# Two passes for a head's output, four softmax scalings on ScalarE, low parts in the taps' queue, late loads and a tail by halves

## The chip, the core and the metric

The kernel runs on one core of a Trainium2 chip: TensorE for matmuls, VectorE, ScalarE, GpSimd and SyncE, with 16 DMA engines between HBM and the core's SBUF. The metric is the device time of one execution in microseconds; less is better.

## The reference

A decoder layer for 512 tokens of width 1024, all in fp32: a gated causal convolution of width 31 and a forgetting attention of 16 heads of 64 side by side, mixed by two gates, then a PEER layer that picks 16 of 16384 experts for each of 8 heads, then a final RMSNorm.

```python
h  = rmsnorm(x, norm1_g)
z  = h @ w_in            # a_val, a_gate, q, k, v, f_logit, g_a, g_b
ya = conformer_conv(a_val, a_gate, conv_w, conv_b, conv_ln_g, conv_ln_b, w_conv_out)
c  = cumsum(log_sigmoid(f_logit + fox_bf))
p  = softmax(where(mask, q @ k.T / 8 + c_q - c_k, NEG));  ob = p @ v      # 16 heads, causal
x  = x + (sigmoid(g_a) * ya + sigmoid(g_b) * (ob @ w_fox_out)) @ w_out
x  = x + peer_ffn(rmsnorm(x, norm2_g), peer_wq, peer_k1, peer_k2, peer_u, peer_v)
return rmsnorm(x, normf_g)
# peer_ffn: u = peer_u[e];  a = gelu(u . h) * gate;  out = sum_k a_k * peer_v[e_k]
```

## The kernel before

An fp32 operand is split into a high and a low part (`hi`, rounded to the matmul's fp32r type, and `lo`, the rest), and `mm3` (L170 to L172) does a product as three matmuls: high by low, low by high, high by high. Weights stream from HBM through SyncE's queue as `wraw`; ScalarE writes `whi` (L125), VectorE subtracts to `wlo` (L129). Every engine works through its instructions in the order in which the program issues them.

The stages, in the time of the profile: v and the first norm (0 to 66 us); the first GLU, q and k (66 to 92); attention (92 to 340); gates and the rest of the convolution (340 to 429); layer norm, output projections and queries (429 to 675); the u stage, 128 blocks of experts, each 24 matmuls of 384 columns (675 to 1269); the v stage, 128 blocks of 18 matmuls of 512 columns (1269 to 1801); and the tail.

Attention goes by pairs of heads, j = 0 to 7, with a ninth round for what is left. In round j the scores of pair j (L594 to L596), the row maxima `mx` (L600, VectorE), the exponentials (L602, ScalarE) and the scaling of the probabilities `Pt` by `rl` (`norm`, L606 to L612: the blocks listed in `NACT` on ScalarE, the others on VectorE) alternate with the transposes of pair j-1 (`tp` L623, split into `pth` on ScalarE and `ptl` on VectorE, L628 and L629) and its outputs (`pvmm`). In between `fill` puts projection steps of round j+1 (q and k in `qk_steps`, the GLU in `glu_steps`). What follows a matmul on other engines is put off by one step through the list `posts`. The convolution's 240 multiply-adds `y` (L493, the taps) are VectorE's background work: `tick` adds a rate per step (`ATT_R`, `ATT_R0`, `GB_R`) and `bg` issues a tap for each whole unit. Behind attention the taps left over run beside the gates (`GB0` steps), up to the sum of `y` that L756 takes.

In the u stage, `bgrun` hands out VectorE time to two generators after each block: routing with its scatter (one-hot tiles `ohs`, 16 small matmuls for each tile at L1066, copied to `gst` by ScalarE at L1069 and written to `Gd` in HBM), and the gathers of single expert rows (`grow`, first 128 products at L1100, then 128 sums at L1106, `U_BG` us a block). `open_second` drains the scatter, frees its memory and issues the first two loads of G, `load_g` (L1161), on ScalarE's queue. In the v stage the gathers left are spread over the blocks; a pair of blocks takes a product and a split of the coefficients (`a_pair`: L1182, `ah` L204, `al` L206).

Of the kernel before, what the change touches and what calls it, by code (L numbers as in the profile page):

```python
# [16 lines left out]
ALU = mybir.AluOpType  # L17
# [44 lines left out]
U_BG = 1.25  # L62
# [7 lines left out]
NACT = (2, 3)  # L70
# [4 lines left out]
VAHEAD = 9  # L75
GB8 = 8
# [9 lines left out]
def body(ctx, tc, x, xT, w_ct, w_v, w_f, w_co, w_fo, w_o, w_q, keys, pu, pv, pur, vecs, conv_w,  # L86
# [315 lines left out]
    def first(*fs):  # L402
        def fn():
            for f in fs:
# [6 lines left out]
                   first(norm1_row, lambda: next(n1)), first(lambda: next(n1))]  # L411
# [139 lines left out]
    def qk_steps(j):  # L551
# [3 lines left out]
        def qsink(p):  # L555
# [3 lines left out]
            def low():  # L559
                for r, u, f in zip(half, half[::-1], range(2)):  # L560
                    dve.scalar_tensor_tensor(qa[u, f, :], p[r, :], 1.0 / math.sqrt(HD), qa[r, f, :].bitcast(F32),
                                             op0=ALU.mult, op1=ALU.subtract)
                    pool.dma_start(qb[r, f, :], qa[r, f, :])
            posts.append(low)

        def ksink(p):
# [3 lines left out]
            def low():  # L570
                for r, u, f in zip(half, half[::-1], range(2)):
                    dve.tensor_tensor(kb[j % 2][r, f, :], p[r, :], ka[r, f, :].bitcast(F32), op=ALU.subtract)
                    pool.dma_start(ka[u, f, :], ka[r, f, :])
            posts.append(low)
# [763 lines left out]
```

## Time and profile before

| | before |
|---|---|
| median of 3 runs | 1814.32 us (1809.08 to 1818.4) |
| profiled execution | 1813.74 us, its span 1811.5 us |
| TensorE busy | 1759.0 us, 97% |
| VectorE busy | 1507.1 us, 83% |
| ScalarE busy | 876.6 us, 48% |
| GpSimd busy | 395.4 us, 22% |
| bytes moved by DMA | 432.92 MB, mean 239 GB/s |

The span is what the profiler saw from the first instruction to the last; the execution's time has some 2 us around it. Busy shares are means over stages with different limits. A row of a timeline gives the start, the duration, the engine, the line of the code, what is written from what, and in brackets how long the engine stood idle before it and which instruction released it. PE is TensorE, DVE VectorE, ACT ScalarE, POOL GpSimd, SP SyncE. The ends of matmuls are modelled and overlap the next one's start, so the distance between starts is what a matmul costs.

### The profile page before, as it was taken

The page shows a single profiled execution, that of the slowest core. Times are in us where ns is not written, and L with a number is a line of the kernel's source. Part 1 is how long each engine was busy: PE and PEld are TensorE (multiplying, and loading weights), DVE is VectorE, ACT ScalarE, POOL GpSimd, SP SyncE. Part 2 cuts the span into 40 slices and gives each one's busy share as a digit, 9 for nine tenths or more (in the row PEclk, how much of TensorE's full clock was granted, in tenths as well). Part 3 has the DMA queues.
Part 4 walks back from the last instruction along what each step waited for, and adds up shares of the span by engine and source line. Part 5 has one row for each costly group of instructions (what it writes and reads, how often), then busy time and mean ns, then how long its engine had stood idle before and what let it go on. Part 6 is the DMA issues. An engine that isn't in the chain of part 4 may idle for free.

```text
span 1811.5 us, 25347 instructions
## 1 busy us (share of the span) xinstructions
PE 1759.0 (97%) x9261; PEld 1537.6 (85%) x9261; DVE 1507.1 (83%) x2649; ACT 876.6 (48%) x1621; POOL 395.4 (22%) x303
## 2 busy tenths in 40 slices
PE   7999999999999999999999999998999999999997
PEld 6887777787888889999999999998888888788886
DVE  5789999999756599989987987865888888888887
ACT  5665655534624233344379489973333333333333
POOL 0000000000000000013422331224444444344441
PEclk9999999999999999999999999999999999999999
DMA  6332222222344225568889989999999999999994
GB/s 210 110 94 76 82 76 72 69 81 94 105 139 136 72 71 159 173 234 305 301 297 332 327 306 334 325 341 375 377 377 378 388 373 389 362 360 391 373 336 159
DMA packets 164477, 432.92 MB, mean 239 GB/s; under 512 B 13696, under 2 KB 63488, under 8 KB 162304
## 3 DMA queue, kind: packets, MB, share of 16 engines
q1 hardware_dynamic: 111408, 238.58, 38.2%
q0 software_dynamic: 39424, 138.43, 21.3%
q10 hardware_dynamic: 13520, 54.29, 7.9%
q8 instruction: 73, 1.20, 0.3%
q14 instruction: 52, 0.43, 0.1%
HBM read 376.20 MB, written 50.86 MB: 236 GB/s over the span
## 4 chain that ended last, share of the span: by engine, by line
PE 68%; DVE 16%; ACT 8%; DMA 6%; issue 3%; ACTq 0%; SPq 0%; POOL 0%; DVEq 0%
PE mm L170 19%; PE mm L171 19%; PE mm L172 19%; DVE y L493 4%; DVE wlo L129 3%; DMA wraw<-in_pv 2%; ACT whi L125 2%; PE tp L171 2%; PE tp L172 2%; PE tp L170 2%; PE pvp L1066 2%; DVE x L1106 2%; ACT ohs L1057 1%; DMA wraw<-in_pu 1%; DVE ptl L629 1%
## 5 line engine op out<-in xcount | busy, mean ns | idle before, releaser
L129 DVE TENSOR_TENSOR wlo<-wraw,whi 128x1024 fp32r<-128x1024 f32 (+1 forms) x434 | 432.5, 1004 | 98.1 <-ACT whi L125 94.4
L125 ACT ACTIVATE whi<-wraw 128x1024 fp32r<-128x1024 f32 (+1 forms) x429 | 373.9, 892 | 100.4 <-DMA wraw<-in_pv 38.9
L170 PE MATMUL mm<-h2h,wlo 128*128 128x384 f32 (+1 forms) x1152 | 398.1, 346 | 8.3 <-DVE wlo L129 7.7
L171 PE MATMUL mm<-h2l,whi 128*128 128x384 f32 (+1 forms) x1152 | 392.8, 341 | 0.5 <-DVE h2l L206 0.5
L172 PE MATMUL mm<-h2h,whi 128*128 128x384 f32 (+1 forms) x1152 | 393.0, 341 | 0.0
L1087 POOL DMA_INDIRECT grow<-in_pur,sx x128 | 181.8, 1421 | 602.5 <-DVE grow L1100 351.8
L1087 POOL DMA_INDIRECT grow<-in_pv,sx x128 | 190.0, 1484 | 236.7 <-DVE x L1106 219.6
L170 PEld LDWEIGHTS mm<-h2h,wlo 128*128 128x128 f32 x1152 | 216.9, 188 | 13.8 <-DVE wlo L129 8.4
L171 PEld LDWEIGHTS mm<-h2l,whi 128*128 128x128 f32 x1152 | 217.0, 188 | 5.7 <-DVE h2l L206 1.1
L172 PEld LDWEIGHTS mm<-h2h,whi 128*128 128x128 f32 x1152 | 216.7, 188 | 5.4
L171 PE MATMUL mm<-wlo,ah 128*128 128x512 f32 x512 | 202.1, 395 | 1.8 <-DVE wlo L129 1.7
L170 PE MATMUL mm<-whi,al 128*128 128x512 f32 x512 | 200.0, 391 | 1.1 <-DVE al L206 1.1
L172 PE MATMUL mm<-whi,ah 128*128 128x512 f32 x512 | 200.1, 391 | 0.0
L204 ACT ACTIVATE ah<-Sb 128x768 fp32r<-128x768 f32 x60 | 50.8, 846 | 292.8 <-DVE Sb L1182 264.6
L493 DVE SCALAR_TENSOR_TENSOR y<-z,cw,y 128x512 f32<-128x512 f32 x240 | 174.6, 746 | 1.0 <-ACT y L490 0.2
L1106 DVE SCALAR_TENSOR_TENSOR x<-grow,dots,x 128x1024 f32<-128x1024 f32 x128 | 164.2, 1283 | 0.9
L170 PE MATMUL mm<-hTh,wlo 128*128 128x512 f32 x384 | 161.7, 421 | 2.2 <-ACT Pt L602 1.6
L1100 DVE SCALAR_TENSOR_TENSOR grow<-grow,hd 128x1024 f32<-128x1024 f32 x128 | 155.2, 1217 | 0.8 <-DMA grow<-in_pur,sx 0.8
L172 PE MATMUL mm<-hTh,whi 128*128 128x512 f32 x384 | 151.1, 393 | 0.0
L171 PE MATMUL mm<-hTl,whi 128*128 128x512 f32 x384 | 150.5, 392 | 0.0
L1141 ACT ACTIVATE gel<-mm 128x384 f32<-128x384 f32 x118 | 57.4, 487 | 172.9 <-PE mm L172 108.2
L1057 ACT ACTIVATE ohs<-ohs,gl 128x128 f16<-128x128 f16 x384 | 118.8, 438 | 11.4 <-DVE ohs L1052 11.3
(280 smaller groups left out, 2914.5 us busy)
## 6 DMA issues: line engine op xcount, KB each, us to landing
wraw<-in_pu SPq DMA_DIRECT2D x128, 512.0 KB
wraw<-in_pv SPq DMA_DIRECT2D x128, 512.0 KB
wraw<-in_w_ct SPq DMA_DIRECT2D x48, 512.0 KB
Gd<-gst SPq DMA_DIRECT2D x24, 1024.0 KB
G<-Gd ACTq DMA_DIRECT2D x16, 1536.0 KB
Sb<-Sd ACTq DMA_DIRECT2D x60, 384.0 KB
Sd<-gel SPq DMA_DIRECT2D x59, 384.0 KB
wraw<-in_w_q SPq DMA_DIRECT2D x16, 512.0 KB
```

Source lines behind the costliest of these rows:

```text
L125: nc.scalar.activation(hi[:, nh * q:hi_to * q], raw[:, nh * q:hi_to * q], AF.Copy)
L129: eng.tensor_tensor(lo[:, c], raw[:, c], hi[:, c].bitcast(F32), op=ALU.subtract)
L170: nc.tensor.matmul(o, ll, rh, start=first, stop=False)
L171: nc.tensor.matmul(o, lh, rl, start=False, stop=False)
L172: nc.tensor.matmul(o, lh, rh, start=False, stop=last)
L204: nc.scalar.activation(hi, src, AF.Copy, scale=1.0 if scale is None else scale)
L493: dve.scalar_tensor_tensor(acc, z[:, w:w + S], cw[:, j, w:w + 1], acc, op0=ALU.mult, op1=ALU.add)
L1057: nc.scalar.activation(o[:, 3, g, :, t], o[:, 1, g, :, t], AF.Copy, scale=gl32[:, t0 + u:t0 + u + 1])
L1087: pool.indirect_dma_start(out=t, out_offset=None, in_=src, in_offset=bass.IndirectOffsetOnAxis(ap=sx[:, n % NG:n % NG + 1], axis=0))
L1100: yield 1.25, dve.scalar_tensor_tensor(t, t, 1.0, hd, op0=ALU.mult, op1=ALU.mult, accum_out=dots[:, k:k + 1])
L1106: yield 1.28, dve.scalar_tensor_tensor(o, t, dots[:, k:k + 1], o, op0=ALU.mult, op1=ALU.add)
L1141: nc.scalar.activation(gel[c][:, n, :], p[:, :TD], AF.Gelu_apprx_tanh)
```

## The change

Six edits, all in one program.

1. v is stored as one tensor `vv` in which a head's 64 high and 64 low columns stand side by side. `pvmm` multiplies each block of it by `ptl` and by `pth`: two matmuls for each of four key blocks instead of three. The output's upper and lower 64 rows have to be added: ScalarE copies one half (`other`), VectorE adds the other (`add`), and the pair's output is then split in one piece of 128 rows (`high` and a low part).
2. `NACT` lists all four blocks, so ScalarE does all scalings of `Pt`.
3. The low parts of q, k and of the output go into a list `lows` which `bg` empties ahead of the taps; `fill` runs the posts before the tick. Rates go from 1.06, 0.7 and 1.3 to 1.32, 0.95 and 1.4.
4. 14 matmuls of a constant stand at the program's start, and the first norm's row is moved one step later.
5. In the u stage `U_BG` goes from 1.25 to 1.15, one scatter tile is kept back while routing runs, and the loads of G and the extra gather buffers come four blocks after `open_second` (`VWAIT`).
6. The last two v blocks run merged by halves of a tile, with sums, scalings and stores by halves, and one half of the last tile is scaled on ScalarE.

```diff
-ATT_R = 1.06
-ATT_R0 = 0.7
+ATT_R = 1.32
+ATT_R0 = 0.95
-GB_R = 1.3
+GB_R = 1.4
-U_BG = 1.25
+U_BG = 1.15
-NACT = (2, 3)
+NACT = (0, 1, 2, 3)
+VWAIT = 4
...
+    wp = pv_ps()
+    for _ in range(NWARM):
+        nc.tensor.matmul(wp[:, :P], onesm, onesm, start=True, stop=True)
...
-                   first(norm1_row, lambda: next(n1)), first(lambda: next(n1))]
+                   first(), first(norm1_row, lambda: next(n1))]
...
+    lows = []
     def bg(n):
         for _ in range(n):
-            if not next(cg, False):
+            if lows:
+                lows.pop(0)()
+            elif not next(cg, False):
                 return
...
-    def pvmm(o, j, pth):
+    def pvmm(o, j, f, pth):
         for kb in range(NT):
             c = slice(OFFK[kb], OFFK[kb] + (NT - kb) * P)
-            mm3(o[:, kb * P:], (v_hi[:, j, kb, :], v_lo[:, j, kb, :]), (pth[0][:, c], pth[1][:, c]),
-                kb == 0, kb == NT - 1)
+            w = vv[:, j, kb, f].rearrange("p a c -> p (a c)")
+            for a in (1, 0):
+                nc.tensor.matmul(o[:, kb * P:], w, pth[a][:, c], start=kb == 0 and a == 1, stop=kb == NT - 1 and a == 0)
...
+        def high():
+            nc.scalar.activation(obT[0][:, j, :], t, AF.Copy)
+            lows.append(lambda: dve.tensor_tensor(obT[1][:, j, :], t, obT[0][:, j, :].bitcast(F32), op=ALU.subtract))
+        def add():
+            dve.tensor_tensor(t[r, :], o[half[0], :], t[r, :], op=ALU.add)
+            if f:
+                posts.append(high)
+        def other():
+            nc.scalar.activation(t[r, :], o[half[1], :], AF.Copy)
+            posts.append(add)
+        posts.append(other)
...
-                if next(gen, 1) is None:
-                    tick(0.65, rate)
+                more = next(gen, 1) is None
                 for fn in todo:
                     fn()
+                if more:
+                    tick(0.65, rate)
...
-        for g in range(GLD - 1):
-            load_g(g)
...
-        if later:
+        if len(later) > busy:
...
+        if vp and b == min(opened + VWAIT, NK - KEEP * SB2 + 1):
+            vready.append(1)
+            for g in range(GLD - 1):
+                load_g(g)
...
+    for i in range(1, NT):
+        k = slice((i - 1) * P, i * P)
+        for f, d in enumerate(halves):
+            for n, (hi, lo) in enumerate(wl):
+                mm3(oacc[i - 1][f], (ah[:, n, k], al[:, n, k]), (hi[:, d], lo[:, d]), False, n == SB2 - 1)
+            if f == 0:
+                scale(i - 1)
+            residual(i, f)
+            if i < NT - 1 and f:
+                for g in range(2):
+                    store(i - 1, g)
```

VectorE in the middle of an attention pair, from the reciprocal `rl` of a pair's first head on; before:

```order
L606 RECIPROCAL rl<-lsum 128x4
L612 TENSOR_SCALAR Pt<-Pt,rl 128x128
L612 TENSOR_SCALAR Pt<-Pt,rl 128x256
L493 SCALAR_TENSOR_TENSOR y<-z,cw,y 128x512
L600 TENSOR_REDUCE mx<-mm 128x1
L493 SCALAR_TENSOR_TENSOR y<-z,cw,y 128x512
L129 TENSOR_TENSOR wlo<-wraw,whi 128x512
```

and after, at the same place:

```order
L617 RECIPROCAL rl<-lsum 128x4
L611 TENSOR_REDUCE mx<-mm 128x1
L583 TENSOR_TENSOR kb<-mm,ka 64x512 x2
L131 TENSOR_TENSOR wlo<-wraw,whi 128x512
L501 SCALAR_TENSOR_TENSOR y<-z,cw,y 128x512
```

The two scalings are gone, the two low parts of k (`kb`), which stood ahead of `rl`, now stand behind it, and the taps have moved behind `wlo`.

ScalarE at the same place, from the high parts of k (`ka`) to the `whi` that `wlo` waits for; before:

```order
L568 ACTIVATE ka<-mm 64x512 x2
L610 ACTIVATE Pt<-Pt,rl 128x384
L610 ACTIVATE Pt<-Pt,rl 128x512
L580 ACTIVATE qb<-y,seld 64x512 x2
L125 ACTIVATE whi<-wraw 128x512
```

and after:

```order
L580 ACTIVATE ka<-mm 64x512 x2
L621 ACTIVATE Pt<-Pt,rl 128x128
L621 ACTIVATE Pt<-Pt,rl 128x256
L621 ACTIVATE Pt<-Pt,rl 128x384
L621 ACTIVATE Pt<-Pt,rl 128x512
L591 ACTIVATE qb<-y,seld 64x512 x2
L127 ACTIVATE whi<-wraw 128x512
```

Two more scalings stand ahead of `qb` and `whi`.

ScalarE around the first loads of G in the u stage, before:

```order
L1141 ACTIVATE gel<-mm 128x384
L1069 ACTIVATE gst<-pvp 128x128x4 x2
L1161 DMA G<-Gd 128x3072 x2
L125 ACTIVATE whi<-wraw 128x1024
L1141 ACTIVATE gel<-mm 128x384
```

and after:

```order
L1094 ACTIVATE gst<-pvp 128x128x4 x2
L127 ACTIVATE whi<-wraw 128x1024
L1166 ACTIVATE gel<-mm 128x384
L127 ACTIVATE whi<-wraw 128x1024
L1166 ACTIVATE gel<-mm 128x384
L127 ACTIVATE whi<-wraw 128x1024
L1166 ACTIVATE gel<-mm 128x384
L127 ACTIVATE whi<-wraw 128x1024
L1166 ACTIVATE gel<-mm 128x384
L1186 DMA G<-Gd 128x3072 x2
```

The two loads have moved behind four more blocks' `whi` and `gel`.

## Rows read from the trace of the kernel before

**Rows 1.** Busy time of each engine by stretch: the stretch in us, its length, then busy us (and instructions) of PE, PEld, DVE, ACT and POOL, the granted clock of TensorE as a share, DMA share and GB/s. An attention pair, the stretch behind attention, two stretches at the opening of the second stage, and the v stage.

```profile
199.19:233.13 33.94, 32.15 (x166) 25.80 (x165) 31.64 (x60) 20.13 (x46) 2.05 (x4) 1.00 0.27 77
340.30:428.90 88.60, 86.66 (x403) 71.80 (x401) 85.28 (x136) 32.61 (x59) 0.00 (x0) 1.00 0.23 78
...
1228.00:1238.00 10.00, 8.47 (x40) 8.47 (x41) 6.93 (x9) 3.36 (x6) 7.81 (x6) 0.76 0.98 385
1238.00:1269.00 31.00, 30.95 (x179) 30.63 (x178) 18.94 (x24) 10.80 (x15) 9.82 (x7) 1.00 1.02 409
1268.90:1800.60 531.70, 528.79 (x2305) 431.51 (x2304) 459.03 (x450) 180.24 (x200) 226.09 (x153) 1.00 0.95 359
```

**Rows 2.** The chain of waits over two attention pairs, 199 to 268 us: the shares by engine and line, then pieces as start, us, and what.

```profile
by line: DVE y L493 31.2%; DVE wlo L129 10.6%; DVE ptl L629 8.3%; DVE mx L600 7.4%; ACT Pt L610 5.4%; issue 4.3%; ACT qb L580 4.2%; DVE qa L561 4.0%; DVE v_lo L673 4.0%; DVE kb L572 3.8%; ACT qa L557 3.5%; ACT whi L125 3.4%; ACT v_hi L668 3
...
203.14 0.66 DVE y L493
...
233.13 1.23 ACT Pt L610 x2
```

**Rows 3.** VectorE's timeline at the two ends of a head's softmax, in mid-pair (198.92 to 202.45) and at a pair's end (214.31 to 216.50).

```profile
198.92 0.18 DVE L606 RECIPROCAL rl<-lsum 128x4 f32<-128x4 f32 x1
199.13 0.55 DVE L612 TENSOR_SCALAR Pt<-Pt,rl 128x128 f32<-128x128 f32 x2
...
202.45 0.69 DVE L129 TENSOR_TENSOR wlo<-wraw,whi 128x512 fp32r<-128x512 f32 x1 [1.12 <-ACT whi L125]
...
214.31 0.17 DVE L606 RECIPROCAL rl<-lsum 128x4 f32<-128x4 f32 x1
...
216.50 0.69 DVE L129 TENSOR_TENSOR wlo<-wraw,whi 128x512 fp32r<-128x512 f32 x1
```

**Rows 4.** ScalarE's timeline, the `whi` at the pair's end.

```profile
215.71 0.61 ACT L125 ACTIVATE whi<-wraw 128x512 fp32r<-128x512 f32 x1
```

**Rows 5.** ScalarE's groups in attention, 92 to 340.3 us, by shape: busy us, mean ns of one, and the idle time before them.

```profile
L610 ACT ACTIVATE Pt<-Pt,rl 128x512 f32<-128x512 f32 x15 | 10.6, 709 | 0.0
...
L610 ACT ACTIVATE Pt<-Pt,rl 128x384 f32<-128x384 f32 x15 | 9.3, 617 | 25.3 <-DVE rl L606 25.3
```

**Rows 6.** VectorE's groups of the same stretch.

```profile
L129 DVE TENSOR_TENSOR wlo<-wraw,whi 128x512 fp32r<-128x512 f32 x58 | 39.8, 687 | 10.5 <-ACT whi L125 10.3
...
L561 DVE SCALAR_TENSOR_TENSOR qa<-mm,qa 64x512 fp32r<-64x512 f32 x14 | 9.6, 689 | 2.7 <-ACT qa L557 2.6
...
L612 DVE TENSOR_SCALAR Pt<-Pt,rl 128x256 f32<-128x256 f32 x15 | 5.2, 348 | 0.0
...
L612 DVE TENSOR_SCALAR Pt<-Pt,rl 128x128 f32<-128x128 f32 x15 | 4.3, 287 | 0.5
```

**Rows 7.** TensorE's timeline: the first matmul of a head's output and the first matmul behind its twelve.

```profile
234.15 0.39 PE L170 MATMUL pvp<-pth,v_lo 128*128 128x512 f32 x1
...
236.00 0.39 PE L594 MATMUL mm<-ka,qa 128*128 128x384 f32 x1
```

**Rows 8.** TensorE's waits from 88 to 440 us: what waits, for what, us in total, times, longest.

```profile
PE tp L623 <- DVE ptl L629: 10.2, 7, 2.2
PE pvp L756 <- issue: 1.9, 1, 1.9
```

**Rows 9.** TensorE's timeline at the program's start.

```profile
7.13 0.77 PE L170 MATMUL mm<-whi,xgl 128*128 128x512 f32 x1 [7.13 <-DVE xgl L208]
...
10.78 0.40 PE L172 MATMUL mm<-whi,xgh 128*128 128x512 f32 x1
11.02 0.39 PE L170 MATMUL mm<-whi,xgl 128*128 128x512 f32 x1
...
31.62 2.08 PE L329 MATMUL tp<-ident,rsc 128*128 128x128 f32 x8 [3.12 <-POOL rsc L324]
```

**Rows 10.** TensorE's timeline in the u stage: the two sets of 16 one-hot matmuls of one block.

```profile
978.33 1.10 PE L1066 MATMUL pvp<-ohs 128*128 128x128 f16 x16 [0.86 <-ACT gst L1069]
...
983.98 1.10 PE L1066 MATMUL pvp<-ohs 128*128 128x128 f16 x16 [0.33 <-ACT gst L1069]
```

**Rows 11.** ScalarE's timeline at the opening of the second stage.

```profile
1226.29 0.83 ACTq L1161 DMA_DIRECT2D G<-Gd  x2
1227.16 1.06 ACT L125 ACTIVATE whi<-wraw 128x1024 fp32r<-128x1024 f32 x1 [13.04 <-issue]
```

**Rows 12.** TensorE's timeline there.

```profile
1229.53 0.69 PE L170 MATMUL mm<-h2h,wlo 128*128 128x384 f32 x1 [7.70 <-DVE wlo L129]
...
1233.17 0.33 PE L170 MATMUL mm<-h2h,wlo 128*128 128x384 f32 x1
1233.34 0.33 PE L171 MATMUL mm<-h2l,whi 128*128 128x384 f32 x1
```

**Rows 13.** VectorE's groups in the v stage, 1268.9 to 1800.6 us.

```profile
L1106 DVE SCALAR_TENSOR_TENSOR x<-grow,dots,x 128x1024 f32<-128x1024 f32 x128 | 164.2, 1283 | 0.9
...
L206 DVE TENSOR_TENSOR al<-Sb,ah 128x768 fp32r<-128x768 f32 x60 | 57.5, 958 | 58.2 <-ACT ah L204 58.2
...
L1100 DVE SCALAR_TENSOR_TENSOR grow<-grow,hd 128x1024 f32<-128x1024 f32 x30 | 36.1, 1219 | 0.0
```

**Rows 14.** TensorE's last matmul, from its timeline.

```profile
1800.24 0.39 PE L172 MATMUL tp<-whi,ah 128*128 128x512 f32 x1
```

**Rows 15.** VectorE's last products, from its timeline.

```profile
1804.37 2.78 DVE L1244 SCALAR_TENSOR_TENSOR to<-x,rsf,gfb 128x512 f32<-128x512 f32 x4
```

More of the change, by code (lines that the diff above doesn't have):

```diff
@@ L395, in v_half @@
             j4 = slice(half * 4, half * 4 + 4)
-            split(v_hi[:, j4, i, :], v_lo[:, j4, i, :], acc[i].rearrange("p (j c) -> p j c", c=P), rsc[:, i:i + 1])
+            for f in range(2):
+                split(vv[:, j4, i, f, 0, :], vv[:, j4, i, f, 1, :],
+                      acc[i].rearrange("p (j f c) -> p j f c", f=2, c=HD)[:, :, f, :], rsc[:, i:i + 1])
     def w_ahead(n):
@@ L557, in qsink, with low @@
                 nc.scalar.activation(qa[r, f, :], p[r, :], AF.Copy, scale=1.0 / math.sqrt(HD))
[L559 to L564, printed above, removed]
+            def low(r, u, f):
+                dve.scalar_tensor_tensor(qa[u, f, :], p[r, :], 1.0 / math.sqrt(HD), qa[r, f, :].bitcast(F32),
+                                         op0=ALU.mult, op1=ALU.subtract)
+                pool.dma_start(qb[r, f, :], qa[r, f, :])
+            lows.extend(lambda r=r, u=u, f=f: low(r, u, f) for r, u, f in zip(half, half[::-1], range(2)))
         def ksink(p):
@@ L568, in ksink, with low @@
                 nc.scalar.activation(ka[r, f, :], p[r, :], AF.Copy)
[L570 to L574, printed above, removed]
+            def low(r, u, f):
+                dve.tensor_tensor(kb[j % 2][r, f, :], p[r, :], ka[r, f, :].bitcast(F32), op=ALU.subtract)
+                pool.dma_start(ka[u, f, :], ka[r, f, :])
+            lows.extend(lambda r=r, u=u, f=f: low(r, u, f) for r, u, f in zip(half, half[::-1], range(2)))
         yield from proj_steps(hT, qsink)
@@ L659, in body, with pv_head @@
         run_posts()
+        bg(len(lows))
     pprev, later, got = [], [], []
-    def pv_head(j, pth):
-        got.append(pv_ps())
-        pvmm(got[-1], j, pth)
-        if len(got) == 2:
-            ro = list(zip(half, got))
-            for r, o in ro:
-                nc.scalar.activation(obT[0][r, j, :], o[r, :], AF.Copy)
-            got.clear()
-            def low():
-                for r, o in ro:
-                    dve.tensor_tensor(obT[1][r, j, :], o[r, :], obT[0][r, j, :].bitcast(F32), op=ALU.subtract)
-            posts.append(lambda: posts.append(low))
+    def pv_head(j, f, pth):
+        o = pv_ps()
+        pvmm(o, j, f, pth)
+        if f == 0:
+            got[:] = [base.tile([P, S], F32, tag="sg", name="ob", bufs=2)]
+        t = got[0]
+        r = half[f]
+        def high():
[9 more added lines that the diff above has]
+        posts.append(other)
     for j in range(KD + 1):
@@ L714, in body @@
             if tr:
-                later.append(lambda j=j - 1, t=tr[1]: pv_head(j, t))
+                later.append(lambda j=j - 1, f=f, t=tr[1]: pv_head(j, f, t))
         if j == KD:
@@ L1194, in open_second @@
         vp.append(ctx.enter_context(tc.tile_pool(name="phe", bufs=1, side="right")))
-        for g in range(GLD - 1):
-            load_g(g)
+    vready = []
+    busy = True
     for b in range(UE + 1, NK):
@@ L1204, in body @@
         share = U_BG if ready else 0.0
-        busy = bgrun(room - share, bgr) or later
+        busy = bgrun(room - share, bgr)
+        more = busy or later
         if ready:
-            bgrun(share if busy else U_END, bgg)
-        if not vp and (not busy or b == NK - VAHEAD):
+            bgrun(share if more else U_END, bgg)
+        if not vp and (not more or b == NK - VAHEAD):
             open_second()
+            opened = b
+        if vp and b == min(opened + VWAIT, NK - KEEP * SB2 + 1):
+            vready.append(1)
+            for g in range(GLD - 1):
+                load_g(g)
         if b == NK - KEEP * SB2 + 4:
```

76 lines of the change are left out of this document (38 added, 38 removed).

## The prediction

> **What bounds the kernel now.** I read the stretches first (the windows view), because TensorE's share over the whole run hides that the stretches differ. An attention pair (two heads) takes 33.94 us, in which TensorE is busy 32.15 and VectorE 31.64; neither is full. The stretch behind attention has TensorE at 86.66 of 88.60 us; the v stage has it at 528.79 of 531.70, with DMA at a share of 0.95 [rows 1]. So in attention TensorE's share cannot say who sets the pace, and the second view is the chain of waits over two pairs: its line by engines names VectorE and ScalarE alone, no matmul, and from one pair's scaling of Pt (233.13 us) it leads back through `y`, `wlo` and the like [rows 2]. A pair is a ring of VectorE and ScalarE steps.
>
> The third view is VectorE's timeline at the two places where a head's softmax ends. In mid-pair `rl` starts at 198.92 and `wlo` at 202.45, after a wait of 1.12 us for ScalarE's `whi`. At the pair's end `rl` starts at 214.31 and `wlo` at 216.50, with no wait, though `whi` started only at 215.71 [rows 3, 4]. That is the slack the change spends: ScalarE's detour is already the later one at the first place and just in time at the second.
>
> **Attention.** Two edits pull apart. A head's output falls from 12 matmuls to 8. The 12 take 234.15 to 236.00, 1.85 us [rows 7]; they go in steps of three per width, so two of each three leave 1.23: -0.62 a head, -9.9 us for 16. But 13 of these heads lie where the chain has no matmul, so their saving lengthens TensorE's idle time; I count it only behind attention.
>
> The other edit puts all four scalings of Pt on ScalarE. The two it has take 0.709 and 0.617 us, 0.092 apart for 128 columns [rows 5]; the two new ones are then 0.525 and 0.433. The pair in the chain takes 1.23 rather than 1.33 [rows 2], so 0.1 overlaps at each joint: four take 1.99, or 0.76 more. VectorE loses 0.55 us for two [rows 3].
> - Mid-pair: from `rl` to `wlo` 3.53 + 0.76 = 4.29 us. VectorE now has `rl`, the small maximum and two `kb` in between, 0.2 + 0.2 + 1.39 = 1.80 (the 64-row subtractions take 0.69 each, as the `qa` ones do [rows 6]). It waits 2.49 instead of 1.12: +1.37.
> - Pair end: `whi` ends 2.01 us after `rl` starts (215.71 + 0.61 - 214.31 [rows 3, 4]), then 2.77. In between stand `rl`, the maximum and two taps at 0.66 [rows 2], 1.72: a new wait of 1.05.
> - VectorE's own work: -1.10 for two pairs of scalings, +0.69 for one more 128x512 subtraction (as `wlo` [rows 6]): two adds and one subtraction take the place of two subtractions. -0.41.
> - The waits of `qa` for ScalarE, 2.6 us over the stretch [rows 6], go, since the low parts are queued later: -0.43 a pair.
>
> That is +1.58 a pair, over six full pairs +9.5. Bounds: -8 if VectorE's waits fall into others and TensorE's saving shows after all (below), +14 if the first and last pair pay too and no tap fills a gap.
>
> **Behind attention.** TensorE is the bound. Three heads' outputs fall here or at the border: 3 x 0.62 = 1.9. The one stall, 1.9 us before the matmul of the conv sum (L756) [rows 8], hangs on VectorE, which is busy 85.28 of 88.60 us [rows 1]; in the built order six taps less are left here, 6 x 0.66 = 4 us. Together 3.8; I take -3.5, bounds -4 and -1 (stall stays, one head counts).
>
> **Start.** The first matmuls run 7.13 to 10.78 us in eight steps of 0.46 where 0.24 follow, some 1.7 us that the 14 matmuls at the head could give back. But TensorE later stands 3.12 us before the transposes of the norm (31.62), for `rsc` from GpSimd [rows 9]: lead won earlier is lost there. Moving that step behind more matmuls fills the hole, until the accumulators wait for the split of v. I take -1.5, bounds 0 (all eaten) and -3.1 (the whole hole goes).
>
> **Scatter.** A block that drains two sets of one-hot matmuls stands 0.86 + 0.33 = 1.19 us for ScalarE's `gst` [rows 10]. In the built order seven blocks do so instead of four: 3 x 1.19 = 3.6. I take +3 because three fewer blocks carry any; bounds -1 (one kept back is always ready) and +5.
>
> **Opening of the second stage.** The loads of G are issued on ScalarE's queue at 1226.29, and ScalarE's next `whi` comes after 13.04 us without work [rows 11]; they wait for the last write of G. TensorE stands 7.70 us for it, and then does twelve steps in 3.64 us where 0.17 each follow, 2.04 [rows 12]; the granted clock of these 10 us is 0.76 [rows 1], so part of them ran at 1.2 instead of 2.4 GHz: 1.6 more. Four blocks later the write has long landed. -8.5, bounds -9.3 and 0.
> The row behind the opening has the DMAs at 409 GB/s and a share of 1.02 [rows 1], so they are full there.
> A rule of the Trainium skill speaks against this edit: "DMA: Bandwidth & Descriptors", section "Issuing engines are not separate DMA queues", says that transfers issued from ScalarE, SyncE or GpSimd run on the same 16 DMA engines and interleave, so a load put later only joins the crowd. By that rule this term is 0 and the sum of all terms +5.8, 1819.5; by the rows, in which ScalarE waits 13.04 us for one write and not for bandwidth, it is -8.5. The trace agrees with the rule where it shows the share of 1.02, and no run here shows the loads in another place.
>
> **v stage.** VectorE counts 128 sums and 30 products here [rows 13]; in the built order six products are left over more, 6 x 1.22 = 7.3 us of VectorE, which has 459 us of work in 531.70 and waits 58 us for ScalarE's `ah` [rows 1, 13]. Those waits pay most of it. +0.5, bounds 0 and +7.5.
>
> **Tail.** TensorE's last matmul ends at 1800.63; VectorE's last product ends at 1807.15 (1804.37 + 2.78) [rows 14, 15], 6.5 us later. Now two adds, one product, one product for a store, two short ones of 0.15 and two more for stores follow, six of 0.69 (as `wlo` [rows 6]) and 0.3, less one add that half the tile's matmuls cover: 4.3 to 3.7 us. -2.2, bounds -1 and -2.8.
>
> **Sum.** 9.5 - 3.5 - 1.5 + 3 - 8.5 + 0.5 - 2.2 = -2.7 on the profiled execution's 1813.74 (span 1811.5 and 2.2 around it), which is 0.6 below the median of the runs shown. I forecast 1811.
>
> **Rivals.**
> *TensorE's saving shows.* If VectorE's longer waits only replace other waits (it idles 2.3 us a pair already), the ring is as long as its work, and TensorE, at 32.15 of 33.94, is the next bound. Six and a half pairs lose 1.24 each, 8 us, in place of +9.5: 1811 - 17.5 = 1793.5. For it: TensorE's waits of 10.2 us on `ptl` are few, seven [rows 8]. Against: no matmul in the chain, and the new waits stand in VectorE's own order.
>
> *DMA is the bound from 1228 on (the slower side).* Behind the opening the DMAs move 409 GB/s at a share of 1.02, and 0.95 through the v stage [rows 1]. If they set the pace, the same bytes must still flow, whether TensorE stood or not: the 8.5 us come back, and six more gathers of 0.5 MB are 3 MB, 7.5 us at 409 GB/s. 1811 + 8.5 + 7.5 - 0.5 = 1826.5. It decides once the share stays at 0.99 or above to the end. For it: that share of 1.02, and a margin of only 0.05 in the stage. Against: TensorE is 99% busy there.
> The rule of the Trainium skill named at the opening points this way.
>
> **How the numbers follow.** Runs of this kernel spread by 0.5% (1809.08 to 1818.4), so that is what a measurement can tell from no change: below 1805.2 faster, above 1823.4 slower. The forecast has a chance of 0.53, with a range of its own of 1803 to 1820 (attention +5 to +14, the rest by a few): 0.12 of it faster, 0.39 same, 0.02 slower. TensorE's saving 0.26, all faster. DMA 0.21: 0.17 slower, 0.04 same. Faster 0.38, same 0.43, slower 0.19. The range is 1794 to 1827, from rival to rival.
>
> **What would show it.** In the changed profile: pairs of about 35.5 us, with VectorE waiting 2.5 us for `whi` in mid-pair and 1 us at the end, and TensorE less busy per pair by 1.2 us; no wait before L756's matmul; no stand of 7.7 us around 1220, and no half clock behind it; one-hot stalls above 6 us; TensorE's end 11 us before the span's end shrinking to 9. Pairs of 33 us, or a DMA share of 1 through the v stage, would prove me wrong.

## The result and the profile after

The changed kernel takes 1833.47 us (median of 4 runs, 1830.62 to 1836.06) against 1812.65 for the kernel before (4 runs): a ratio of 1.0108, interval 1.0088 to 1.0127. It is 20.8 us slower; 1811 was forecast, and the range ended at 1827.

The profiled execution has a span of 1830.33 us, 18.9 more than before. Both traces are cut at the same marks: the starts of the first and the last of the sixteen reciprocals `rl`, of the matmul of the conv sum, of the first query matmul and of the first matmul of the v stage, and the end of that stage's last one. The forecast is the terms of the prediction's sum.

| stretch, us | before | after | difference | forecast |
|---|---|---|---|---|
| start to the first `rl` | 106.41 | 107.66 | +1.25 | -1.5 |
| attention, first to last `rl` | 233.91 | 246.58 | +12.67 | +9.5 |
| last `rl` to the conv sum's matmul | 88.57 | 91.59 | +3.02 | -3.5 |
| to the first query matmul | 130.08 | 130.02 | -0.06 | 0 |
| queries and u stage | 709.91 | 706.01 | -3.90 | -5.5 |
| v stage | 531.74 | 539.10 | +7.36 | +0.5 |
| tail | 10.85 | 9.37 | -1.48 | -2.2 |

Two borders move from one execution to the next. The seven profiles with the start of the kernel before take 104.3 to 106.4 us up to the first `rl`, the six with the start of the kernel after 106.4 to 107.9. And of h1 and h2 (below), whose u and v stages are those of before, the v stages take 532.6 and 529.6 us, while both stages together stay within 0.2 us of before's 1241.65. So the u and the v stage are best read together: 3.5 us more than before, where -5.0 was forecast.

First the stretches in numbers, in the columns of [rows 1]: an attention pair, the stretch behind attention, ten microseconds behind the loads of G, and the v stage.

```profile
205.47:241.03 35.56, 31.86 (x157) 24.59 (x156) 31.59 (x59) 21.97 (x51) 2.23 (x5) 1.00 0.26 76
354.24:445.70 91.46, 87.13 (x386) 71.07 (x386) 83.39 (x132) 32.58 (x60) 0.00 (x0) 0.96 0.26 86
1237.00:1247.00 10.00, 10.00 (x60) 10.00 (x59) 5.93 (x7) 4.55 (x6) 6.84 (x6) 1.00 1.02 417
1281.86:1820.96 539.10, 530.50 (x2305) 429.67 (x2304) 467.78 (x467) 181.15 (x204) 232.52 (x161) 1.00 0.95 361
```

The pair is 1.6 us longer than the one in [rows 1] with TensorE and VectorE no busier: the time is waiting. The five full pairs average 35.85 us where they had 34.27. VectorE's timeline shows where, at the two places of [rows 3].

```profile
205.47 0.18 DVE L617 RECIPROCAL rl<-lsum 128x4 f32<-128x4 f32 x1
...
205.74 1.39 DVE L583 TENSOR_TENSOR kb<-mm,ka 64x512 fp32r<-64x512 f32 x2
209.70 0.69 DVE L131 TENSOR_TENSOR wlo<-wraw,whi 128x512 fp32r<-128x512 f32 x1 [2.57 <-ACT whi L127]
...
223.70 0.18 DVE L617 RECIPROCAL rl<-lsum 128x4 f32<-128x4 f32 x1
...
226.45 0.69 DVE L131 TENSOR_TENSOR wlo<-wraw,whi 128x512 fp32r<-128x512 f32 x1 [1.08 <-ACT whi L127]
```

`wlo` waits 2.57 us in mid-pair and 1.08 us at the pair's end; 2.49 and 1.05 were forecast. ScalarE's groups give the price of the two new scalings, 0.497 and 0.405 us (0.525 and 0.433 forecast from [rows 5]), and VectorE's groups the sums: waits of `wlo` from 10.5 to 29.1 us, those of `qa` from 2.7 to 0.4 [rows 6]. First ScalarE, then VectorE, 95 to 354 us:

```profile
L621 ACT ACTIVATE Pt<-Pt,rl 128x512 f32<-128x512 f32 x15 | 10.7, 712 | 0.0
...
L621 ACT ACTIVATE Pt<-Pt,rl 128x256 f32<-128x256 f32 x15 | 7.5, 497 | 0.0
...
L621 ACT ACTIVATE Pt<-Pt,rl 128x128 f32<-128x128 f32 x15 | 6.1, 405 | 26.8 <-DVE rl L617 26.8
```

```profile
L131 DVE TENSOR_TENSOR wlo<-wraw,whi 128x512 fp32r<-128x512 f32 x58 | 39.9, 688 | 29.1 <-ACT whi L127 28.9
...
L573 DVE SCALAR_TENSOR_TENSOR qa<-mm,qa 64x512 fp32r<-64x512 f32 x14 | 9.6, 689 | 0.4
```

TensorE's waits from 88 to 446 us have changed their kind [rows 8]: the wait for the conv sum is gone, and new ones stand for `qa`, for the exponentials, and one of 3 us for a `ptl` (us in total, times, longest).

```profile
PE tp L634 <- DVE ptl L640: 6.8, 8, 3.1
PE mm L605 <- ACT Pt L613: 6.1, 5, 2.1
PE mm L172 <- DVE qa L573: 5.8, 5, 1.6
...
PE pvp L650 <- DVE ptl L640: 3.0, 1, 3.0
```

That last one is in the ninth round. In TensorE's timeline it is followed by matmuls 0.4 to 0.5 us apart instead of 0.23; the granted clock of the 6 us from 387.1 on is 0.53, so that nearly all of them ran at the lower of its two levels (1.2 and 2.4 GHz).

```profile
387.10 0.47 PE L650 MATMUL pvp<-ptl,vv 128*128 128x128 f32 x1 [2.95 <-DVE ptl L640]
...
387.59 0.74 PE L172 MATMUL mm<-hTh,wlo 128*128 128x512 f32 x1
388.12 0.63 PE L173 MATMUL mm<-hTl,whi 128*128 128x512 f32 x1
```

At the start TensorE's wait for `rsc` has fallen from 3.12 us [rows 9] to 0.7. The longest of the waits up to 85 us that were not there is for the split of v, which ScalarE and VectorE now do in 16 pieces each instead of 8:

```profile
PE mm L172 <- DVE vv L210: 3.1, 2, 2.7
```

At the opening of the second stage the stand of 13.04 us on ScalarE [rows 11] is gone. What is there now, on ScalarE's timeline, are waits for weights on their way (a median of 12.5 us from issue to landing), and one stand of TensorE behind them where 7.70 us were [rows 12]:

```profile
1237.85 0.83 ACTq L1186 DMA_DIRECT2D G<-Gd  x2
...
1251.04 1.06 ACT L127 ACTIVATE whi<-wraw 128x1024 fp32r<-128x1024 f32 x1 [4.46 <-DMA wraw<-in_pu]
...
1258.56 1.06 ACT L127 ACTIVATE whi<-wraw 128x1024 fp32r<-128x1024 f32 x1 [6.08 <-DMA wraw<-in_pu]
```

```profile
1260.93 0.44 PE L172 MATMUL mm<-h2h,wlo 128*128 128x384 f32 x1 [2.39 <-DVE wlo L131]
```

In the v stage VectorE's groups, in the columns of [rows 13], count 35 products where 30 stood, and the waits for `ah` are the same 58 us. TensorE's matmuls wait for `wlo` 7.8 us in all, where it was 1.7. First VectorE's groups, then TensorE's wait (us in total, times, longest):

```profile
L1131 DVE SCALAR_TENSOR_TENSOR x<-grow,dots,x 128x1024 f32<-128x1024 f32 x128 | 164.5, 1286 | 1.1
...
L208 DVE TENSOR_TENSOR al<-Sb,ah 128x768 fp32r<-128x768 f32 x60 | 57.5, 959 | 58.3 <-ACT ah L206 58.3
...
L1125 DVE SCALAR_TENSOR_TENSOR grow<-grow,hd 128x1024 f32<-128x1024 f32 x35 | 42.1, 1220 | 0.0
```

```profile
PE mm L173 <- DVE wlo L131: 7.8, 17, 0.7
```

At the end the last matmul starts at 1820.57 and VectorE's last product ends at 1825.16, 4.2 us after the matmul's end, where it was 6.5 [rows 14, 15]:

```profile
1820.57 0.39 PE L174 MATMUL tp<-whi,ah 128*128 128x512 f32 x1
```

```profile
1824.41 0.75 DVE L1273 SCALAR_TENSOR_TENSOR to<-x,rsf,gfb 128x512 f32<-128x512 f32 x1 [0.44 <-POOL rsf L1268]
```

### The profile page after: what moved, and what is told of

It reads as the page before. It is cut to its first block, busy times and chain, and to the rows that moved or that the text cites. A ratio compares the mean times of both kernels' runs of the same rounds, so it can differ in the third digit from the quotient of the medians.

```text
span 1830.3 us, 25301 instructions
## 1 busy us (share of the span) xinstructions
PE 1767.8 (97%) x9225; PEld 1533.3 (84%) x9225; DVE 1504.9 (82%) x2633; ACT 895.5 (49%) x1670; POOL 391.6 (21%) x303
## 4 chain that ended last, share of the span: by engine, by line
PE 46%; DVE 25%; ACT 14%; DMA 9%; issue 5%; ACTq 0%; SPq 0%; POOL 0%; POOLq 0%; DVEq 0%
PE mm L172 14%; PE mm L173 14%; PE mm L174 14%; DVE y L501 6%; DMA wraw<-in_pv 6%; DVE wlo L131 6%; DVE x L1131 5%; ACT whi L127 5%; ACT ohs L1082 3%; DMA wraw<-in_pu 2%; ACT ah L206 2%; DVE Sb L1207 2%; PE pvp L1091 2%; ACT Pt L621 2%; DVE ptl L640 1%
## 5 line engine op out<-in xcount | busy, mean ns | idle before, releaser
L127 ACT ACTIVATE whi<-wraw 128x1024 fp32r<-128x1024 f32 (+1 forms) x429 | 374.5, 894 | 90.6 <-DMA wraw<-in_pv 41.0
L1131 DVE SCALAR_TENSOR_TENSOR x<-grow,dots,x 128x1024 f32<-128x1024 f32 x128 | 164.5, 1286 | 1.1
L173 PEld LDWEIGHTS mm<-wlo,ah 128*128 128x128 f32 x512 | 96.1, 188 | 38.0 <-DVE wlo L131 18.9
```

The source lines that it names most:

```text
L127: nc.scalar.activation(hi[:, nh * q:hi_to * q], raw[:, nh * q:hi_to * q], AF.Copy)
L173: nc.tensor.matmul(o, lh, rl, start=False, stop=False)
L1131: yield 1.28, dve.scalar_tensor_tensor(o, t, dots[:, k:k + 1], o, op0=ALU.mult, op1=ALU.add)
```

## The experiments

Stretches of the runs are cut as in the table. The first four undo or repeat parts of the change; edits of one run lie in different stretches. `...` marks what is left out of a diff.

**e1.** After, with `NACT` and `U_BG` as before.

```diff
-U_BG = 1.15
+U_BG = 1.25
...
-NACT = (0, 1, 2, 3)
+NACT = (2, 3)
```

> After with two things undone that lie in different stages: scalings for 128 and 256 columns back on VectorE, U_BG back at 1.25. Ring theory (the scalings' detour through ScalarE sets the attention pair): the two waits of wlo fall from 2.57 and 1.08 us to about 1.2 and 0, and a pair from 35.9 to about 34 us; attention 12 us shorter. Rival (the output's extra copy, add and low part set it): waits fall, but the pair stays above 35.3. v stage: if the six gathers left over are what made it 539.1 instead of 531.7 us, it returns to 532 to 534; if it is the later loads, it stays at 539.

Measured: 1818.67 us, ratio to before 1.0028 (1.0008 to 1.0047). Attention 236.76 instead of 246.58, the pair 34.5 instead of 35.9, and VectorE's waits for `whi` in attention back at 11.5 us:

```profile
L131 DVE TENSOR_TENSOR wlo<-wraw,whi 128x512 fp32r<-128x512 f32 x58 | 39.7, 684 | 11.5 <-ACT whi L127 11.3
```

The ring theory holds, by 9.8 us of the 12 expected. The v stage stayed at 540.0 with 30 products as before, but the u stage fell to 702.0: together 3.1 us less than after. So the place of the loss was open.

**e2.** After, with the old rates, and the second layer's sums at half width.

```diff
-ATT_R = 1.32
-ATT_R0 = 0.95
+ATT_R = 1.06
+ATT_R0 = 0.7
...
-GB_R = 1.4
+GB_R = 1.3
...
-            yield 1.28, dve.scalar_tensor_tensor(o, t, dots[:, k:k + 1], o, op0=ALU.mult, op1=ALU.add)
+            yield 1.28, dve.scalar_tensor_tensor(o[:, :512], t[:, :512], dots[:, k:k + 1], o[:, :512], op0=ALU.mult, op1=ALU.add)
```

> After with the old rates of taps (1.06, 0.7, 1.3); and the sums of gathered rows done on half their width (half of the second layer's gathered sums is left out), DMAs unchanged. Rates: the 2.95 us stand of TensorE near 387 us, and the half clock behind it, go if the denser taps put ptl late; the pair falls by some 2 us since about five taps leave it, and the stretch behind attention grows by 10 to 20 us, as 30 taps more are left for it. v stage: if VectorE bounds it, about 69 us of its work are gone and the stage falls to 522 to 526 us; if DMA bounds it, it stays within 3 us of 539.

Measured: 1814.77 us with that part left out. The v stage is 522.4, and TensorE is busy all of it: 68 us less of VectorE's sums take the stage to TensorE's floor, the least that any run shows. With the old rates pairs fall to 32 us for four rounds, but the next two take 39.3 and 39.7. There TensorE stands 7.7 us at once, and 9.1 us more in front of the conv sum. First the sums (164.5 us in after), then TensorE's waits (us in total, times, longest):

```profile
L1131 DVE SCALAR_TENSOR_TENSOR x<-grow,dots,x 128x512 f32<-128x512 f32 x128 | 96.1, 751 | 1.1
```

```profile
PE mm L605 <- ACT Pt L613: 9.4, 3, 7.7
PE pvp L781 <- issue: 9.1, 1, 9.1
```

Attention is 241.7, 4.9 less than after with ten taps fewer in it, and the stretch behind it 93.8 (+2.2, where 10 to 20 was expected). The stand at 387 us has shrunk to 0.4, but here the taps put off came back as waits.

**e3.** After, with a third matmul for each key block, and every second gathered row of the second half left out.

```diff
-            for a in (1, 0):
-                nc.tensor.matmul(o[:, kb * P:], w, pth[a][:, c], start=kb == 0 and a == 1, stop=kb == NT - 1 and a == 0)
+            for n, a in enumerate((1, 0, 0)):
+                nc.tensor.matmul(o[:, kb * P:], w, pth[a][:, c], start=kb == 0 and n == 0, stop=kb == NT - 1 and n == 2)
...
+        if n >= NG and n % 2:
+            return last[0]
```

> After with a third matmul for each key block of a head's output (the high part of the probabilities is added twice, so the output is another one): 12 matmuls as before, all else as after. Ring theory: the pair grows by less than 0.4 us, attention by under 3. Rival (TensorE's saving counts): +1.2 a pair, +8 us. v stage: odd gathered rows of the second half aren't fetched but take the row before (64 of 128 transfers of 0.5 MB left out), VectorE's work unchanged. If DMA bounds the stage, 32 MB at 385 GB/s, 85 us of DMA, are gone and it falls to 522 to 526 us; if VectorE bounds it, it stays within 3 us of 539.

Measured: 1827.31 us. Attention 246.42 against 246.58: four matmuls more for each head cost nothing there. Behind attention it is even 2.5 us shorter (89.1), as the stand falls to 2.1 us and no drop of the clock follows. The v stage is 534.4, outside both expectations but near VectorE's: 4.7 less for some 85 us of DMA taken away, where e2 gave 16.7 for 68 us of VectorE's work. The DMA share of the stage falls from 0.95 to 0.84, VectorE's work stays (467.8 in after):

```profile
1278.96:1813.38 534.42, 528.81 (x2305) 429.60 (x2304) 466.19 (x467) 179.75 (x204) 147.60 (x97) 1.00 0.84 302
```

**e4.** Before, with two constants of the change.

```diff
-U_BG = 1.25
+U_BG = 1.15
...
-NACT = (2, 3)
+NACT = (0, 1, 2, 3)
```

> Before with only two constants of the change: all four scalings on ScalarE, and U_BG 1.15. Ring theory: in mid-pair wlo waits 2.5 instead of 1.1 us, at the pair's end 1.0 instead of 0, VectorE gives 0.9 back: pairs of 35.5 us, attention 9 to 11 us longer. Rival (the late low parts or the outputs make the pair long): pairs stay at 34 to 34.5. v stage: 537 to 540 us if the gathers left over are the cause, 532 if not.

Measured: 1827.2 us, ratio 1.0064 (1.0039 to 1.009). Attention 242.75, 8.8 more than before; pairs of 35.6; `wlo` waits 2.42 us in mid-pair. The u and v stages together are 6.0 us longer (711.9 and 535.8, between the two expectations for the v stage). Two numbers alone make some three fifths of the loss.

**f1, f2, f4.** e2 and e3 point to VectorE in the v stage, whose waits for `ah` come once a pair of blocks. Here the low part `al` is issued behind the next `wlo`: in before (f1), in after (f2), and in before with the late loads, the tile kept back and the tail by halves (f4).

```diff
-        split(hi, lo, a)
+        nc.scalar.activation(hi, a, AF.Copy)
         As[k] = (hi, lo)
+        lates.append(lambda: dve.tensor_tensor(lo, a, hi.bitcast(F32), op=ALU.subtract))
...
         hi, lo = next_w()
+        while lates:
+            lates.pop(0)()
```

> Before with one thing moved: in the v stage the low part al of a pair's coefficients is issued on VectorE behind the next wlo instead of right behind ah, so that ScalarE's 0.85 us for ah runs beside it. VectorE theory (its work and its waits for ah bound the v stage): the 62 us of waits for ah fall under 10, the stage falls from 531.7 to 522 to 526 us (TensorE's own work is 522), ratio 0.995 to 0.997. DMA theory (weights and gathers at a share of 0.99 bound it): the waits move to whi and wraw, the stage stays at 530 to 533, ratio 1.

> After with the same move of al. VectorE theory: the v stage falls from 539.1 to 523 to 527 us, so that the six gathers more no longer show, and the whole is 12 to 16 us shorter than after. DMA theory: 537 to 541.

> Before with the late loads, the scatter tile kept back, the tail by halves and al behind wlo, U_BG at 1.25; attention as before. VectorE theory: with its waits gone from the v stage the late loads' gain lasts: u stage 5 to 8 us shorter, v stage 522 to 527, tail 1.6 shorter; 12 to 18 us faster than before, ratio 0.990 to 0.993. DMA theory: u stage shorter, v stage 536 to 540, no gain but the tail's, ratio 0.999.

Measured: 1861.45, 1883.96 and 1859.75 us, ratios 1.0266, 1.0394 and 1.0257; v stages of 574.2, 583.0 and 577.2. All three missed, to the other side. VectorE's timeline in f1 says why:

```profile
1502.80 1.22 DVE L129 TENSOR_TENSOR wlo<-wraw,whi 128x1024 fp32r<-128x1024 f32 x1 [1.91 <-ACT whi L125]
1503.94 0.95 DVE L1189 TENSOR_TENSOR al<-Sb,ah 128x768 fp32r<-128x768 f32 x1
```

`al` no longer waits, but `wlo` ahead of it now waits 1.91 us, for `ah` and then `whi` on ScalarE: 0.95 us more a pair of blocks. VectorE's waits over the stage, first two rows of before, then f1's (us in total, times, longest):

```profile
DVE al L206 <- ACT ah L204: 61.1, 63, 1.2
DVE wlo L129 <- ACT whi L125: 7.2, 8, 2.1
...
DVE wlo L129 <- ACT whi L125: 123.6, 63, 6.1
```

That is 55 us more of waiting. Three products fewer are left over here, so VectorE's work is 12 us less (446.8 against 459.0): together +43, and the stage is 42.4 us longer. The other 7 us of f1 stand at the border of the two stages, where the first v matmul waits 8.2 us for the first pair's `al`. The DMAs fall to a share of 0.95 meanwhile, where the same 100 us of before have 0.99:

```profile
1400.00:1500.00 100.00, 93.17 (x400) 73.91 (x399) 78.49 (x73) 30.52 (x33) 40.57 (x28) 1.00 0.95 350
```

What VectorE gains or loses goes into the stage's time with hardly any cover. Had DMA set the pace before, part of it would have been covered.

**f3.** Before, with the late loads alone.

```diff
-        for g in range(GLD - 1):
-            load_g(g)
...
+        if vp and b == min(opened + VWAIT, NK - KEEP * SB2 + 1):
+            vready.append(1)
+            for g in range(GLD - 1):
+                load_g(g)
```

> Before with the late loads alone (G loaded and the extra gather buffers used four blocks after the opening). If the 7.7 us stand is a gain that lasts: 7 to 9 us faster, ratio 0.996. VectorE theory (from the last write of G on, VectorE's work and waits set the end): the u stage is 7 to 9 us shorter, the v stage 5 to 9 us longer, the whole within 3 us of before.

Measured: 1809.67 us, ratio 0.9973 (0.9956 to 0.999). The u stage is 4.6 us shorter, the v stage 1.1 longer: 3.6 us less by the profile, 4.9 by the ratio, where 8.5 was booked. That lies between the two theories. e1's expectation had named the later loads as the cause if the v stage stayed at 539; alone they do not make it longer by more than 1.1.

**g1 and g4.** The low part the right way round, behind the gathered sums of its block and ahead of `wlo`: in before (g1) and in after (g4).

```diff
-        split(hi, lo, a)
+        nc.scalar.activation(hi, a, AF.Copy)
         As[k] = (hi, lo)
+        lates.append(lambda: dve.tensor_tensor(lo, a, hi.bitcast(F32), op=ALU.subtract))
...
-        hi, lo = next_w()
-        ah, al = As[c]
...
             if next(bgg, None) is None:
                 break
+        while lates:
+            lates.pop(0)()
+        hi, lo = next_w()
+        ah, al = As[c]
```

> Before with al moved the other way: behind the gathered sums of its block and ahead of the next wlo, so that a sum of 1.28 us runs on VectorE while ScalarE makes ah, and whi has its time too. f1 showed that each 0.95 us of VectorE wait more per pair of blocks comes out of the stage (531.7 to 574.1). VectorE theory, the other sign: the 62 us of waits for ah fall under 10 and the v stage from 531.7 to 522 to 526 us, where TensorE's 522 is the floor; ratio 0.995 to 0.997. DMA theory: the waits turn into waits for whi, the stage stays at 529 to 533.

> After with al behind the sums and nothing else. VectorE theory: the v stage falls from 539.1 to 522 to 527 us though its gathers and loads are those of after, and the whole by 12 to 16 us to some 1819. DMA theory: 535 to 540.

Measured: g1 1803.58 us, ratio 0.9949 (0.9929 to 0.9969), v stage 523.4; g4 1815.2 us, v stage 522.4 with the gathers and loads of after. In g1's timeline of VectorE two sums run where the wait was:

```profile
1502.18 2.60 DVE L1106 SCALAR_TENSOR_TENSOR x<-grow,dots,x 128x1024 f32<-128x1024 f32 x2
1505.05 0.96 DVE L1189 TENSOR_TENSOR al<-Sb,ah 128x768 fp32r<-128x768 f32 x1 [0.27 <-ACT ah L1187]
```

```profile
1400.00:1500.00 100.00, 100.00 (x443) 82.84 (x442) 88.91 (x80) 35.05 (x37) 41.72 (x30) 1.00 1.01 393
```

TensorE is busy all of these 100 us. The waits for `ah` fell to 40 us only, not under 10, but they no longer count, since TensorE now sets the pace. DMA at a share of 1.01 does not hold this stage up.

**g2.** The version that beats both: before with the late loads, the tail by halves and `al` behind the sums.

> Before with three edits: late loads, tail by halves, al behind the sums. If the three add up: u stage 704 to 706 (as f3), v stage 522 to 526, tail 9.3 to 9.5; 12 to 15 us faster than before, ratio 0.992 to 0.9935. If DMA is the floor behind the late loads: v stage 530 or more, ratio 0.996 to 0.998.

Measured: 1798.01 us (5 runs), ratio 0.9917 (0.99 to 0.9934). u stage 703.3, v stage 523.0, tail 9.4. The three add up: 4.9 us (f3), 9.2 (g1) and 1.5 for the tail are 15.6, and 14.8 were measured.

**g3.** After, mended.

```diff
-        rate = ATT_R if j else ATT_R0
+        rate = ATT_R if 0 < j < KD else ATT_R0 if not j else 0.6
...
-        if len(later) > busy:
+        if later:
```

> After with four things mended: scalings for 128 and 256 columns on VectorE, U_BG 1.25, no tile kept back, al behind the sums, and in the ninth attention round a tap rate of 0.6 instead of 1.32. Last round: if the denser taps put the last ptl late, the 2.95 us stand near the round's end and the half clock go, and the stretch from the last rl to the conv sum's matmul falls from 91.6 (89.9 in e1) to 84 to 87 us; if it comes from the two-pass output itself, the stand stays. Attention as e1: 236 to 237. v stage 522 to 526. The whole 5 to 14 us faster than before, ratio 0.992 to 0.997.

Measured: 1807.65 us, ratio 0.9965 (0.9952 to 0.9978). Attention 236.75 and v stage 522.5 as expected. The stand on `ptl` is gone, but the stretch behind attention stays at 90.2, not 84 to 87, since the taps put off are now waited for in front of the conv sum:

```profile
PE pvp L781 <- issue: 6.2, 1, 6.2
```

**h1 and h2.** What is left of attention: two edits, each alone in the kernel before. h1 has the two-pass output (the diff's `vv`, `pvmm` and `pv_head`, its low part through `posts`), h2 the list `lows`, the order in `fill` and the three rates.

> Before with the two-pass output alone (v side by side, 8 matmuls a head, copy, add, one split of 128 rows; its low part through the old posts). The saving of 9.9 us of TensorE counts: attention 226 to 229 us instead of 233.9, ratio 0.996. Ring theory: VectorE has one more 128x512 subtraction a pair (0.6 us) and no wait goes: attention 234 to 238, and behind it at most 2 us less; ratio 0.999 to 1.002.

> Before with the late low parts alone: the low parts of q and k in the taps' queue, posts ahead of the tick, rates 1.32, 0.95 and 1.4. If these cost what is left of attention (e1: +2.85 us with the scalings back on VectorE): attention 236 to 238, and the stand of 2.95 us in the last round shows here. If the two-pass output costs it: attention 232 to 234 (the waits of qa, 2.3 us, gone), no stand.

Measured: h1 1814.07 us, ratio 1.0002 (0.9985 to 1.0018), attention 232.90 (-1.0, outside both expectations but near the ring theory's), behind it 87.5 (-1.1). h2 1815.94 us, ratio 1.0017 (1.0001 to 1.0033), attention 238.49 (+4.6), behind it 87.7 (-0.9). In h2 TensorE's waits in attention have a row that before did not have:

```profile
PE mm L170 <- DVE qa L565: 8.7, 5, 2.2
```

That row does not explain the 4.6 us, since TensorE does not set the pace there (e3). Attention is VectorE's work and its idle time, and every wait of VectorE that the profiles of the two name there is for ScalarE: 215.1 us of work and 18.8 of idle time before, 221.4 and 17.1 in h2. So h2's waits fell, and its work grew. What grew are the taps. VectorE's groups of attention, before, h2, after and e2:

```profile
L493 DVE SCALAR_TENSOR_TENSOR y<-z,cw,y 128x512 f32<-128x512 f32 x143 | 105.0, 745 | 0.0
...
L493 DVE SCALAR_TENSOR_TENSOR y<-z,cw,y 128x512 f32<-128x512 f32 x154 | 112.3, 745 | 0.2 <-ACT y L490 0.2
...
L501 DVE SCALAR_TENSOR_TENSOR y<-z,cw,y 128x512 f32<-128x512 f32 x149 | 109.1, 746 | 0.1
...
L501 DVE SCALAR_TENSOR_TENSOR y<-z,cw,y 128x512 f32<-128x512 f32 x139 | 99.6, 741 | 0.0
```

The higher rates bring h2 eleven taps more and after six, and taking the rates back alone takes ten out of after and 4.9 us off its attention (e2). That is as much as h2 costs in all, which leaves the late low parts little share; they were not tried without the rates. The two-pass output saves 2 of its 9.9 us: in h1 TensorE is busy 6.9 us less in attention (214.6 for 221.5) and attention is 1.0 shorter. The start takes that back: 107.3 us, where the kernels with before's start have 105.5 on average. The three edits' single effects, 8.8 (e4), 4.6 (h2) and -1.0 (h1), sum to 12.4, against 12.67 in after. Of the stand in the ninth round h1 has 0.2 us and h2 0.8; only both together have it.

## Why the prediction was wrong

It goes by the prediction's own steps. Every stretch that the change touches came out slower than its term. Of the 21.6 us between forecast and profile the v stage has 6.9, the stretch behind attention 6.5, attention 3.2, the start 2.8, the u stage 1.6 and the tail 0.7.

- **Attention, the scalings.** Right, in place and size: waits of 2.57 and 1.08 us (2.49 and 1.05), and +1.30 a full pair in e4, where 1.37 + 1.05 - 1.10 = 1.32 was booked. Over the stretch they cost 8.8 us (e4) to 9.8 (e1).
- **Attention, the other edits.** The pair came out at +1.58, as booked, but by luck in this part. The two-pass output was booked at +0.69 a pair and takes off 0.2 (h1). The low parts were booked at -0.43, for the waits of `qa`: these do go (2.7 to 0.4 us over the stretch), but the taps that come with the rates make it +0.7 (h2). Together they are +0.23 in e1, where +0.26 was booked: two errors that cancel.
- **Attention, the edges.** The sum took six full pairs. The five that are full gave 7.9 us, the first pair 1.2, the last 3.1 with three taps more than before, the rest 0.4. That is the case of the bound of +14.
- **The taps.** "Six taps less are left here" was booked behind attention, at -4 us, and nowhere in attention, where the six went: a term put at nothing. They are there (148 for 142, and 76 for 82 behind it), at some 0.75 us each.
- **The two-pass output.** "Their saving lengthens TensorE's idle time" held: 12 matmuls or 8 make no difference in attention (e3), and the edit alone gives 1.0 us there (h1). The rival of TensorE's saving falls. The sign that TensorE would be 1.2 us less busy a pair did not show: 31.86 against 32.15.
- **Behind attention.** The step "TensorE is the bound" failed. Before, VectorE's 85 us of work and 2.5 of waits for ScalarE fill 88 of the 88.6 us. The stall of 1.9 us went as booked, but the new stand of 2.95 us for a `ptl` queued among denser taps, with the lowered clock behind it, gave +3.02 where -3.5 was booked. g3 takes the stand away and gets it back as 6.2 us in front of the conv sum: both engines bind here.
- **Start.** The bound that the prediction named as end of the gain, the accumulators' wait for the split of v, took more than the lead: 3.1 us of wait, +1.25, or +1.9 by the means of the profiles above. The split alone is enough for it: h1 has it without the matmuls at the head, and takes 107.3 us.
- **Opening, scatter and `U_BG`.** Together with the v stage +3.5 for -5.0, and the runs part this in three. The late loads are worth -3.6 (f3), where -8.5 was booked. For the rest +3 (the scatter's stalls) and +0.5 (the products) were booked. Of it `U_BG` costs +3.1 by the difference of after and e1, and 6.0 alone (e4), and what e1 has beyond f3, the tile kept back and the tail by halves, +3.9 (4.3 by f4 and f1). One-hot stalls grew by only 1.4 us (6.7 for 4.9 and 0.4). -3.6 + 3.1 + 3.9 is +3.4.
- **The tail's edit in the v stage.** The 3.9 us come within the v stage: e1 is 3.3 us ahead of f3 at its start, 2.3 behind at its block 64 and 3.8 behind at block 120. There the tail by halves spreads the same 158 gathers over 124 blocks instead of 126. By block 120 that is 2.4 gathers of 1.28 us more, 3.1 us of VectorE's work, an estimate from these counts. It fits, but the edit was not tried without the kept-back tile.
- **Opening.** The step that failed is that TensorE's stand and the lowered clock behind it would come back whole. The stand of 7.70 went, but 2.39 came behind it with weights 12.5 us on their way, and VectorE set the pace of what follows. The Trainium skill's rule ("DMA: Bandwidth & Descriptors", section "Issuing engines are not separate DMA queues") made this term 0: the trace agrees with its crowd (share 1.02 before and after, `whi` waiting 6.08 us for a weight), but the 13.04 us of ScalarE behind one write are gone, and 3.6 us of gain remain. With the v stage no longer on VectorE, the late loads and the tail by halves together take 5.4 us off the two stages (g2 against g1).
- **v stage.** The step "those waits pay most of it" failed: they paid nothing, 58.2 us before and 58.3 after. VectorE's 459 us of work and its 58 us of waits for `ah` made 517 of 531.7 us in the rows already: it had next to no slack to pay with, as each wait stands in its own queue and comes again with each pair. Its work grew by 8.8 us, and the stage by 7.4. Of that work five products are 6 us; but e1, with 30 products and a stage of 540.0, shows that they are not all of the 7.4: the tail's edit and the moving border have their part. f1 shows the bound with more waiting (+42 us), e2 with less work, g1 and g4 with the wait filled. The Trainium skill's page "Perfetto Trace Analysis", section "Identifying the Most-Contended Engine", has VectorE's busy share as a fair measure of its distance from its limit; here that was 86% with TensorE at 99%, and the runs decide for VectorE. The Trainium skill says on the same page that VectorE and ScalarE are strict in their order (section "Tensor Engine Instruction (MATMUL, LD_WEIGHTS)"), which f1 shows: `wlo` waits 1.91 us behind `ah` on ScalarE.
- **Tail.** -1.5 for -2.2. VectorE's part came as booked: its last product ends 4.2 us after the last matmul where it was 6.5, though it waits 0.44 us for GpSimd's power. From there to the end of the span it is 5.2 us instead of 4.3, with the last stores under way; why was not tried.
- **The slower rival.** "DMA is the bound from 1228 on" gave 1826.5 and falls for the v stage: some 85 us less of DMA gave 4.7 us (e3), and at a share of 1.01 TensorE was busy throughout (g1). By its own sign, a share of 0.99 or above to the end, it was not met either: 0.95.

Not settled: how the new stand in the ninth round arises from two edits that hardly show it apart, how the 3.9 us divide between the kept-back tile and the tail by halves, and what the late low parts do without the rates.

## What to carry to other kernels

Add an in-order engine's work and its recurring waits before calling it idle: an engine that is 86% busy and waits for a neighbour in each round can set the pace of one that is 99% busy, and then an instruction added to it is paid nearly in full. Fill such a wait with an independent instruction that is already at hand, ahead of the next dependency: moved behind another wait, the instruction makes that wait longer (f1, 42 us in the stage); moved behind ready work, it brings the stage within 1 us of TensorE's floor (g1, 8.4 us less). When work leaves the engine that is not the bound, look for what the edit adds to the one that is. And work that an edit moves from one stretch to another has to be booked in both.

## What was not expected of the hardware

The same stand of 2.95 us, in the same place of the same program part, was followed by 6 us at a granted clock of 0.53 in one execution (after) and of 0.72 in three (e1, f2, g4); after a stand of 2.1 us (e3) the stretch kept 1.00. What the clock does behind a stand is not the same from one execution to the next: f2 and g4 have after's code up to there, and took 90.6 us behind attention where after took 91.6. The length of attention is the same: 233.86 to 233.91 us in the six profiles that share its code with before, and 246.39 to 246.58 in after, f2 and g4.
